# One of the four weight sums of each group made by an adding transfer that GpSimd begins

## The chip, the cores and the metric

The kernel runs on one core of one Trainium2 chip. The core has five engines that this text speaks of by these names: TensorE (PE in the profile; its weight loads are PEld), VectorE (DVE), ScalarE (ACT), GpSimd (POOL) and SyncE (SP), which here only begins transfers. Sixteen DMA engines move the data. Each engine works through its own list of instructions in order; semaphores make one wait for another.

The metric is the device time of one execution in microseconds. Three runs of the kernel before took 2479.81, 2481.71 and 2482.42 us; their median is 2481.71 us.

## The reference

Two blocks of a transformer are computed on 512 tokens of width 1024, in float32. Of the first block only the two SwiGLU layers matter here (the first layer of the block and the third):

```python
def swiglu(y, w_gate, w_up, w_down):
    return (jax.nn.silu(y @ w_gate) * (y @ w_up)) @ w_down
```

`w_gate` and `w_up` are 1024 x 2816, `w_down` is 2816 x 1024. Between the two SwiGLU layers stands a token mixer with two recurrences (mLSTM and HGRN2). The second block has a neighbourhood attention, a differential attention, two convolutional feed-forward layers and two small gated layers.

## The kernel before, in words

**Every float32 product is three fast products.** A weight tile is rounded to a fast format (`wh`, by ScalarE) and the rest is kept beside it (`wl`, by VectorE); activations are split the same way into `yh` and `yl`. TensorE then adds up wh·yh, wh·yl and wl·yh.

**The gate and up products of the SwiGLU layers** save a multiplication of blocks: `seven` forms a block of 256 output rows by seven products of half blocks instead of eight (Strassen's scheme). For that the weights must be summed beforehand. `sums_w` does this for one group, that is 256 columns of one matrix. The four quarters of the group are a, b, c and d (each 128 x 512 in SBUF), and the sums are s1 = c + d, s2 = s1 - a, s3 = a - c and s4 = b - s2. A group takes three tiles of the pool `wraw` (tag `wr`, four buffers): x[0] holds a and s1, x[1] holds s2 and b, x[2] holds d and c; s3 takes c's place and s4 takes a's. Three transfers on SP's queue bring c and d (one of 512 KB), a and b (256 KB each). VectorE makes the four sums. Then the halves of (a, s1), (s2, b), (d, s3) and (s4) are written into the pool `wts` (tags `wh` and `wl`, six buffers each): that is what TensorE reads.

A group is 7 x 4 x 3 = 84 multiplications of 256 columns. In each of the two SwiGLU layers there are 19 such groups (one block of `w_gate` is done in the ordinary way), so 38 in all. After every second block pair (four groups), `partial` multiplies by a part of `w_down`: four ordinary weight tiles with 24 multiplications of 512 columns each. Those tiles pass through the same `wr` and `wts` buffers.

**What sets the order.** All operations are first recorded with tiles as dependencies. `deadlines` works backwards from an estimated time for each TensorE operation and gives every other operation a latest start; a transfer's is moved forward by 40 us more (`DMA_AHEAD`). It also orders the tiles of the first-come pools (`wr`, `wh`, `wl`, `ps`) by when they are first due. `schedule` then runs a list scheduler with fixed prices, picks on each engine the operation that is due first and whose buffers are free, and `emit` writes the instructions out in that order. Every engine's list is therefore fixed at build time: an instruction that waits on the chip holds back all that stand behind it on its engine. All instructions written by `emit` carry one line (L514 before, L515 after).

`SLOTS` fixes how many buffers each pool has; the pool `acts` holds activations of 128 x 516 floats and has 56.

Of the kernel before, what the change touches and what calls it, by code (L numbers as in the profile page):

```python
# [13 lines left out]
ALU = mybir.AluOpType  # L14
# [25 lines left out]
class Tile_:  # L40


    def __init__(self, rec, pool, tag, shape, dt, name):
        self.rec, self.pool, self.tag, self.shape, self.dt, self.name = rec, pool, tag, list(shape), dt, name
        self.real = None
        self.uses = 0
        self.acc = []
        n = int(np.prod(shape[1:]))
        self.np = np.lib.stride_tricks.as_strided(rec.dummy, (shape[0], n), (rec.width, 1)).reshape(shape) if len(shape) == 2 else None
        self.made = False  # L50
        self.turn = None
        self.n = None
        self.last = None


class View:
# [116 lines left out]
DMA_AHEAD = 40000.0  # L173
# [13 lines left out]
class Recorder:  # L187
# [59 lines left out]
    def add(self, eng, fn, args, kw):  # L247
        o = Op()
        o.i, o.eng, o.fn, o.args, o.kw = len(self.ops), eng, fn, args, kw
        views = [a for a in list(args) + list(kw.values()) if isinstance(a, View)]  # L250
        out = kw.get("out", args[0] if args else None)
        outs = [v for v in (out, kw.get("accum_out")) if isinstance(v, View)]
        ins = [v for v in views if not any(v is w for w in outs)]
        if fn in ("copy_predicated",) or (fn == "matmul" and not kw.get("start")):
            ins = ins + [outs[0]]
        o.cost = self.price(eng, fn, outs[0] if outs else None, args, kw, ins)
        o.lat = 0.0
# [4 lines left out]
        if fn == "dma_start":  # L262
            v = outs[0] if outs else ins[0]
# [8 lines left out]
        if eng == "tensor":  # L272
            t = outs[0].t
# [29 lines left out]
    def deadlines(self, slots, when):  # L303

        ops = self.ops
        late = {}
        tiles = {}
        for o in ops:
            for t in o.tiles:
                if t.pool in self.psum:  # L310
                    q = tiles.setdefault(t.tag, [])
                    if t.n is None:
                        t.n = len(q)
                        q.append(o)
                    t.end = o
        need = {}
        for o in ops:
            for t in o.tiles:
                if t.pool in self.psum and t.end is o:
                    q = tiles[t.tag]  # L320
                    j = t.n + slots[t.pool, t.tag]
                    if j < len(q):
                        need[o.i] = min(need.get(o.i, 1e18), when[q[j].i] - 230)
        for o in reversed(ops):
            end = min([late[u.i] - WAIT[o.eng][u.eng] - (SLACK.get(o.outn.split("_")[0], SLACK[""]) if o.eng != u.eng else 0.0) for u in o.users] + [need.get(o.i, 1e18)], default=1e18)
            if o.fn == "dma_start":
                end -= 2100 + DMA_AHEAD
            s = end - o.cost
            if o.eng == "tensor":
                s = min(s, when[o.i])  # L330
            elif s > 1e17:
                s = when[o.i] + 20000.0
            if o.fn == "dma_start":
                s = o.pr if not o.users or o.kept else min(s, o.pr)
            late[o.i] = o.pr = s
        first = {}
        for o in reversed(ops):
            for x in o.tiles:
                first[id(x)] = late[o.i]
        for q in self.fifo.values():  # L340
            for i, x in enumerate(sorted(q, key=lambda x: first[id(x)])):
                x.turn = i

    def schedule(self, slots, reserve):
# [11 lines left out]
        tfree = dict.fromkeys(engs, 0.0)  # L356
# [12 lines left out]
        now = 0.0  # L369
        done = 0  # L370
        n = len(ops)
# [20 lines left out]
        while done < n:  # L392
# [4 lines left out]
            for e in engs:  # L397
# [3 lines left out]
                while w and w[0][0] <= now:  # L401
                    _, i, o = heapq.heappop(w)
# [4 lines left out]
                while r:  # L407
                    x = heapq.heappop(r)
                    o = x[2]
# [29 lines left out]
                o = pick  # L439
# [10 lines left out]
                c = o.cost  # L450
# [9 lines left out]
                if o.fn == "dma_start":  # L460
                    s = max(now + 500, dma_free)
                    dma_free = s + c
                    o.end = dma_free + 1600
                    tfree[e] = now + 450
                else:
                    o.end = now + c
                    tfree[e] = o.end
# [29 lines left out]
            now = min(nxt)  # L497
# [17 lines left out]


SLOTS = {
    ("acts", "a"): 56, ("wraw", "wr"): 4, ("pads", "pad"): 3, ("wts", "wh"): 6, ("wts", "wl"): 6,
    ("pmm", "mm"): 4, ("pat", "at"): 2, ("paux", "aux"): 2,
}  # L520
RESERVE = {("acts", "a"): 12}
# [29 lines left out]
class Builder:  # L551
# [169 lines left out]
    def sums_w(self, key, g):  # L721

        nc = self.nc
        W = self.I["s_" + key[0]][g]
        n = 4 * P
        nc.offset = -LOOK_DMA
        x = [nc.tile("wraw", "wr", [P, WP], F32, self.nm("wr"), True) for _ in range(3)]
        h = slice(0, n), slice(n, 2 * n)
        a, s1, s2, b, d, c = [t[:, i] for t in x for i in h]
        nc.sync.dma_start(out=x[2][:, 0:2 * n], in_=W[:, 2 * n:4 * n])  # L730
        nc.sync.dma_start(out=a, in_=W[:, 0:n])
        nc.sync.dma_start(out=b, in_=W[:, n:2 * n])
        nc.offset = -LOOK_PREP
        forms = {}

        def halves(t, names):
            hi = nc.tile("wts", "wh", [P, WP], F32R, self.nm("wh"), True)
# [4 lines left out]
                nc.scalar.copy(out=hi[:, i], in_=t[:, i])  # L742
                nc.vector.tensor_tensor(out=lo[:, i], in0=t[:, i], in1=hi[:, i].bitcast(F32), op=ALU.subtract)

        nc.vector.tensor_tensor(out=s1, in0=c, in1=d, op=ALU.add)
        nc.vector.tensor_tensor(out=s2, in0=s1, in1=a, op=ALU.subtract)
        nc.vector.tensor_tensor(out=c, in0=a, in1=c, op=ALU.subtract)
        halves(x[0], ("a", "s1"))
# [1144 lines left out]
```

## Time and profile before

| what | value |
|---|---|
| median of three runs | 2481.71 us |
| the profiled execution | 2484.38 us |
| its span | 2482.6 us |
| granted TensorE clock, mean share | 0.991 |
| PE busy | 2403.4 us (97%) |
| DVE busy | 1838.7 us (74%) |
| ACT busy | 1159.6 us (47%) |
| POOL busy | 459.3 us (18%) |
| moved by DMA | 270.37 MB, 109 GB/s |

The span is the time from the first to the last instruction of the program; 1.8 us of the profiled execution lie around it. A busy share is an average over stages with different limits. In rows of the trace, "ps", "wh", "wr" and so on are tiles without their buffer numbers; "idle before" is how long an engine stood still just before an instruction, with the instruction or transfer that ended the wait.

### The profile page before, as it was taken

The page shows a single profiled execution, that of the slowest core. Times are in us where ns is not written, and L with a number is a line of the kernel's source. Part 1 is how long each engine was busy: PE and PEld are TensorE (multiplying, and loading weights), DVE is VectorE, ACT ScalarE, POOL GpSimd, SP SyncE. Part 2 cuts the span into 40 slices and gives each one's busy share as a digit, 9 for nine tenths or more (in the row PEclk, how much of TensorE's full clock was granted, in tenths as well). Part 3 has the DMA queues.
Part 4 walks back from the last instruction along what each step waited for, and adds up shares of the span by engine and source line. Part 5 has one row for each costly group of instructions (what it writes and reads, how often), then busy time and mean ns, then how long its engine had stood idle before and what let it go on. Part 6 is the DMA issues. An engine that isn't in the chain of part 4 may idle for free.

```text
span 2482.6 us, 37567 instructions
## 1 busy us (share of the span) xinstructions
PE 2403.4 (97%) x14452; PEld 2107.3 (85%) x14452; DVE 1838.7 (74%) x3100; ACT 1159.6 (47%) x2084; POOL 459.3 (18%) x549
## 2 busy tenths in 40 slices
PE   9999999998999999989999999999999999999999
PEld 6899999987789999987779888789877788888788
DVE  8988878873768877787887872667888879744567
ACT  5544444142535444546665442334565565433343
POOL 1000003000130000055543210113223223100122
PEclk9999999999999999999999999999999999999999
DMA  9644444574225433422322323233312223333322
GB/s 332 210 154 151 132 124 84 114 157 99 94 58 172 137 103 102 153 65 64 93 62 78 111 94 94 93 95 109 99 49 84 67 77 102 94 94 97 93 93 75
DMA packets 227925, 270.37 MB, mean 109 GB/s; under 512 B 10769, under 2 KB 191249, under 8 KB 227746
## 3 DMA queue, kind: packets, MB, share of 16 engines
q1 hardware_dynamic: 227746, 267.98, 35.9%
q8 instruction: 113, 1.85, 0.3%
q14 instruction: 66, 0.54, 0.1%
HBM read 261.62 MB, written 10.51 MB: 110 GB/s over the span
## 4 chain that ended last, share of the span: by engine, by line
PE 40%; DVE 7%; issue 2%; ACT 1%; POOL 1%; POOLq 0%; DVEq 0%; ACTq 0%
PE ps L514 36%; DVE wl L514 1%; DVE P L514 1%; PE sc L514 1%; PE po L514 1%; DVE z L514 1%; DVE h L514 1%; DVE ul L514 1%; DVE Kl L514 1%; PE pt L514 1%; ACT P L514 0%; POOL P L514 0%; PE ss L514 0%; POOL rsq L514 0%; DVE yl L514 0%
## 5 line engine op out<-in xcount | busy, mean ns | idle before, releaser
L514 PE MATMUL ps<-yl,wh 128*128 128x256 f32 (+1 forms) x2528 | 793.1, 321 | 6.3 <-DVE yl L514 6.2
L514 PE MATMUL ps<-yh,wh 128*128 128x256 f32 (+1 forms) x2528 | 784.5, 321 | 13.7 <-ACT yh L514 8.0
L514 PE MATMUL ps<-yh,wl 128*128 128x256 f32 (+1 forms) x2528 | 787.7, 320 | 0.0
L514 DVE TENSOR_TENSOR wl<-wr,wh 128x1024 fp32r<-128x1024 f32 x466 | 562.2, 1210 | 231.0 <-ACT wh L514 228.9
L514 ACT CAST wh<-wr 128x1024 fp32r<-128x1024 f32 x466 | 468.5, 1012 | 534.6 <-PE ps L514 387.9
L514 PEld LDWEIGHTS ps<-yh,wh 128*128 128x128 f32 x2528 | 472.1, 190 | 54.2 <-ACT yh L514 11.7
L514 PEld LDWEIGHTS ps<-yl,wh 128*128 128x128 f32 x2528 | 474.1, 190 | 47.1 <-DVE yl L514 12.1
L514 PEld LDWEIGHTS ps<-yh,wl 128*128 128x128 f32 x2528 | 474.2, 190 | 34.4
L514 PE MATMUL ps<-uh,wh 128*128 128x512 f32 (+1 forms) x1336 | 481.8, 367 | 9.8 <-DVE z L514 7.4
L514 PE MATMUL ps<-ul,wh 128*128 128x512 f32 (+1 forms) x1336 | 484.1, 366 | 3.8 <-DVE ul L514 3.8
L514 PE MATMUL ps<-uh,wl 128*128 128x512 f32 (+1 forms) x1336 | 483.4, 366 | 0.0
L514 POOL TENSOR_TENSOR sq<-sq,sq 128x256 f32<-128x256 f32 (+1 forms) x150 | 137.1, 917 | 841.6 <-ACT sq L514 838.8
L514 PEld LDWEIGHTS ps<-uh,wh 128*128 128x128 f32 x1336 | 250.2, 189 | 50.1 <-issue 3.0
L514 PEld LDWEIGHTS ps<-ul,wh 128*128 128x128 f32 x1336 | 252.1, 189 | 42.6 <-DVE ul L514 4.3
L514 PEld LDWEIGHTS ps<-uh,wl 128*128 128x128 f32 x1336 | 251.7, 189 | 38.4
L514 POOL TENSOR_TENSOR cx<-cx,cv 128x512 f32<-128x512 f32 x44 | 76.5, 1758 | 558.7 <-DVE cv L514 535.6
L514 DVE TENSOR_TENSOR z<-z,ps 128x256 f32<-128x256 f32 (+1 forms) x176 | 88.8, 513 | 103.3 <-PE ps L514 102.6
L514 DVE SCALAR_TENSOR_TENSOR ada<-ada,scb 128x1024 f32<-128x1024 f32 x72 | 88.5, 1234 | 24.7 <-DMA ada<-in_adaT_dram 24.6
L514 POOL TENSOR_SCALAR P<-P,sm 128x256 f32<-128x256 f32 (+2 forms) x96 | 72.9, 777 | 140.2 <-DVE sm L514 115.0
L514 ACT ACTIVATE P<-P,mx 128x512 f32<-128x512 f32 (+2 forms) x128 | 81.1, 635 | 31.9 <-DVE mx L514 25.7
L514 ACT ACTIVATE sq<-z 128x256 f32<-128x256 f32 x112 | 45.6, 416 | 96.5 <-DVE z L514 95.9
L514 DVE TENSOR_TENSOR wr<-wr 128x512 f32<-128x512 f32 x114 | 78.3, 687 | 6.3 <-DMA wr<-in_s_ffn_w_up_dram 4.3
(238 smaller groups left out, 3163.3 us busy)
## 6 DMA issues: line engine op xcount, KB each, us to landing
wr<-in_ffn_w_in_dram SPq DMA_DIRECT2D x88, 512.0 KB, 3.6
ada<-in_adaT_dram SPq DMA_DIRECT2D x72, 512.0 KB, 6.4
wr<-in_ffn_w_down_dram SPq DMA_DIRECT2D x44, 512.0 KB, 4.3
wr<-in_ffn_w_out_dram SPq DMA_DIRECT2D x44, 512.0 KB, 3.4
wr<-in_w_in_dram SPq DMA_DIRECT2D x32, 512.0 KB, 9.1
wr<-in_na_w_qkv_dram SPq DMA_DIRECT2D x24, 512.0 KB, 3.9
wr<-in_da_w_qkv_dram SPq DMA_DIRECT2D x24, 512.0 KB, 3.8
wr<-in_s_ffn_w_up_dram SPq DMA_DIRECT2D x20, 512.0 KB, 4.2
```

Source lines behind the costliest of these rows:

```text
L514: getattr(getattr(nc, o.eng), o.fn)(*[real(a) for a in o.args], **{k: real(v) for k, v in o.kw.items()})
```

## The change

In `sums_w` the sum s1 = c + d is no longer made by VectorE. SP loads d a second time, into the place of s1, and then GpSimd begins a transfer that reads c from memory a second time and adds it to what lies there (`accum_op=ALU.add`). That transfer reads and writes s1, so it is ordered behind the load of d into s1. Each group now reads 512 KB more.

Three things go with it. The three tiles of a group are made "mates": in the order of the `wr` pool they stand together, in the place of the one that is due first, so x[0], x[1], x[2] now follow one another, where x[2] came first. A transfer begun by GpSimd gets its own price and latest start. And the memory set aside for the lists of transfers that GpSimd writes grows from 1024 to 4096 (`dynamic_dma_scratch_size`), while the pool `acts` shrinks from 56 to 54 buffers.

```diff
@@ class Tile_
         self.last = None
+        self.mates = [self]
@@ Recorder.add
-        if fn in ("copy_predicated",) or (fn == "matmul" and not kw.get("start")):
+        if fn in ("copy_predicated",) or (fn == "matmul" and not kw.get("start")) or "accum_op" in kw:
             ins = ins + [outs[0]]
@@ Recorder.deadlines
             if o.fn == "dma_start":
-                end -= 2100 + DMA_AHEAD
+                end -= 2100 + (DMA_AHEAD if o.eng == "sync" else 1000)
...
-            if o.fn == "dma_start":
+            if o.fn == "dma_start" and o.eng == "sync":
                 s = o.pr if not o.users or o.kept else min(s, o.pr)
...
-            for i, x in enumerate(sorted(q, key=lambda x: first[id(x)])):
+            for i, x in enumerate(sorted(q, key=lambda x: min(first[id(y)] for y in x.mates))):
@@ Recorder.schedule
-                    tfree[e] = now + 450
+                    tfree[e] = now + (450 if e == "sync" else 1000)
@@ SLOTS
-    ("acts", "a"): 56, ("wraw", "wr"): 4, ("pads", "pad"): 3, ("wts", "wh"): 6, ("wts", "wl"): 6,
+    ("acts", "a"): 54, ("wraw", "wr"): 4, ("pads", "pad"): 3, ("wts", "wh"): 6, ("wts", "wl"): 6,
@@ Builder.sums_w
         x = [nc.tile("wraw", "wr", [P, WP], F32, self.nm("wr"), True) for _ in range(3)]
+        for t in x:
+            t.t.mates = [v.t for v in x]
...
         nc.sync.dma_start(out=x[2][:, 0:2 * n], in_=W[:, 2 * n:4 * n])
+        nc.sync.dma_start(out=s1, in_=W[:, 2 * n:3 * n])
         nc.sync.dma_start(out=a, in_=W[:, 0:n])
         nc.sync.dma_start(out=b, in_=W[:, n:2 * n])
         nc.offset = -LOOK_PREP
         forms = {}
+        nc.gpsimd.dma_start(out=s1, in_=W[:, 3 * n:4 * n], accum_op=ALU.add)
...
-        nc.vector.tensor_tensor(out=s1, in0=c, in1=d, op=ALU.add)
         nc.vector.tensor_tensor(out=s2, in0=s1, in1=a, op=ALU.subtract)
@@ kernel
-    nc = bacc.Bacc("TRN2", target_bir_lowering=False, num_devices=1, dynamic_dma_scratch_size=1024)
+    nc = bacc.Bacc("TRN2", target_bir_lowering=False, num_devices=1, dynamic_dma_scratch_size=4096)
```

The first place is VectorE's list in the middle of the first SwiGLU layer, where one group (x[0] to x[2] are wr_1573, wr_1597, wr_1540) ends and the next (wr_1713, wr_1722, wr_1632) begins. Before:

```order
L514 TENSOR_TENSOR wr_1540<-wr_1573,wr_1540 128x512
L514 TENSOR_TENSOR z_999<-z_999,ps_1637 128x512
L514 TENSOR_TENSOR z_1004<-z_1004,ps_1661 128x512
L514 TENSOR_TENSOR wr_1573<-wr_1597 128x512
L514 TENSOR_TENSOR wl_1711<-wr_1540,wh_1697 128x1024
L514 TENSOR_TENSOR wr_1713<-wr_1632 128x512
L514 TENSOR_TENSOR wr_1722<-wr_1713 128x512
L514 TENSOR_TENSOR z_1038<-z_1038,ps_1699 128x512
L514 TENSOR_TENSOR z_1043<-z_1043,ps_1704 128x512
L514 TENSOR_TENSOR wl_1754<-wr_1573,wh_1741 128x512
L514 TENSOR_TENSOR wr_1632<-wr_1713,wr_1632 128x512
```

VectorE's list at the same place, with the groups (wr_1563, wr_1580, wr_1606) and (wr_1638, wr_1722, wr_1730), now:

```order
L515 TENSOR_TENSOR wr_1606<-wr_1563,wr_1606 128x512
L515 TENSOR_TENSOR z_1006<-z_1006,ps_1642 128x512
L515 TENSOR_TENSOR z_1012<-z_1012,ps_1668 128x512
L515 TENSOR_TENSOR wr_1563<-wr_1580 128x512
L515 TENSOR_TENSOR wl_1719<-wr_1606,wh_1705 128x1024
L515 TENSOR_TENSOR wr_1722<-wr_1638 128x512
L515 TENSOR_TENSOR z_1035<-z_1035,ps_1707 128x512
L515 TENSOR_TENSOR z_1046<-z_1046,ps_1712 128x512
L515 TENSOR_TENSOR wl_1758<-wr_1563,wh_1749 128x512
L515 TENSOR_TENSOR wr_1730<-wr_1638,wr_1730 128x512
```

The sum s1 (wr_1713<-wr_1632 before) is gone; s2 (wr_1722<-wr_1638) and s3 (wr_1730<-wr_1638,wr_1730) keep their places.

SP's list for the same groups, with two tiles of `w_down` ahead, before:

```order
L514 DMA wr_1506<-in_ffn_w_down_dram 128x4x256
L514 DMA wr_1540<-in_s_ffn_w_gate_dram 128x1024
L514 DMA wr_1573<-in_s_ffn_w_gate_dram 128x512
L514 DMA wr_1597<-in_s_ffn_w_gate_dram 128x512
L514 DMA wr_1632<-in_s_ffn_w_up_dram 128x1024
L514 DMA wr_1713<-in_s_ffn_w_up_dram 128x512
L514 DMA wr_1722<-in_s_ffn_w_up_dram 128x512
```

SP's list at the same place, now ("x2" is the load of d into s1 and the load of a):

```order
L515 DMA wr_1499<-in_ffn_w_down_dram 128x4x256
L515 DMA wr_1563<-in_s_ffn_w_gate_dram 128x512 x2
L515 DMA wr_1580<-in_s_ffn_w_gate_dram 128x512
L515 DMA wr_1606<-in_s_ffn_w_gate_dram 128x1024
L515 DMA wr_1638<-in_s_ffn_w_up_dram 128x512 x2
L515 DMA wr_1722<-in_s_ffn_w_up_dram 128x512
L515 DMA wr_1730<-in_s_ffn_w_up_dram 128x1024
```

x[0] now takes the first buffer that comes free and x[2], with c and d, the last.

GpSimd's list around the start of the second SwiGLU layer, now: before, the first DMA row and the eighteen that follow the last `rsq` here were not there.

```order
L515 TENSOR_TENSOR sq_7410<-sq_7410,sq_7530 128x256
L515 DMA wr_7491<-in_s_ffn_w_up_dram 128x512
L515 TENSOR_TENSOR rsq_7628<-ms_7620,mhalf 128x2
L515 TENSOR_TENSOR sq_7663<-sq_7663,sq_7669 128x256
L515 TENSOR_TENSOR sq_7663<-sq_7663,sq_7686 128x256
L515 TENSOR_TENSOR sq_7663<-sq_7663,sq_7692 128x256
L515 TENSOR_TENSOR sq_7663<-sq_7663,sq_7709 128x256
L515 TENSOR_TENSOR sq_7663<-sq_7663,sq_7715 128x256
L515 TENSOR_TENSOR rsq_7767<-ms_7761,mhalf 128x2
L515 DMA wr_8233<-in_s_ffn_w_gate_dram 128x512
```

One adding transfer stands ahead of a reciprocal root (`rsq`); in the first layer all 19 stand in one piece with no other work of GpSimd among them. Outside the SwiGLU layers the lists are the same but for two stretches, one in each attention of the second block, where PE, ACT and DVE have some of their rows in another order.

## Rows read from the trace of the kernel before

**Rows 1.** The page's busy line: us, share of the span, instructions.
```profile
PE 2403.4 (97%) x14452; PEld 2107.3 (85%) x14452; DVE 1838.7 (74%) x3100; ACT 1159.6 (47%) x2084; POOL 459.3 (18%) x549
```

**Rows 2.** Stretches: busy us of PE, PEld, DVE, ACT, POOL; PEclk, DMA share, GB/s.
```profile
0.00:73.00 73.00, 65.06 (x255) 47.92 (x256) 61.55 (x118) 39.50 (x59) 10.09 (x10) 1.00 0.95 332
...
100.00:300.00 200.00, 200.00 (x1379) 185.52 (x1378) 173.54 (x265) 89.05 (x137) 0.00 (x0) 1.00 0.47 155
...
690.00:780.00 90.00, 84.42 (x652) 80.59 (x650) 73.81 (x149) 45.17 (x85) 21.41 (x24) 0.96 0.41 119
780.00:1040.00 260.00, 259.67 (x1834) 242.67 (x1835) 208.25 (x301) 126.32 (x195) 0.00 (x0) 1.00 0.37 118
1160.00:1260.00 100.00, 96.60 (x500) 78.22 (x501) 80.48 (x170) 64.13 (x149) 55.62 (x65) 1.00 0.25 76
1850.00:1950.00 100.00, 97.33 (x527) 80.33 (x526) 85.56 (x182) 60.87 (x121) 28.28 (x22) 1.00 0.26 82
```

**Rows 3.** Timeline of PE in a group: start, duration; first and 27th row.
```profile
199.81 0.29 PE L514 MATMUL ps<-yl,wh 128*128 128x256 f32 x1
...
202.88 0.28 PE L514 MATMUL ps<-yh,wh 128*128 128x256 f32 x1
```

**Rows 4.** Timeline of PE in a tile of w_down, four starts apart.
```profile
149.01 0.39 PE L514 MATMUL ps<-yh,wh 128*128 128x512 f32 x1
...
149.94 0.40 PE L514 MATMUL ps<-yl,wh 128*128 128x512 f32 x1
```

**Rows 5.** Waits, 100 to 300 us: total us, times, longest.
```profile
ACT wh L514 <- PE ps L514: 70.3, 35, 5.0
...
DVE wr L514 <- DMA wr<-in_s_ffn_w_up_dram: 4.3, 3, 1.4
```

**Rows 6.** Tile wr, 100 to 300 us: durations min/median/max in ns.
```profile
L514 ACT CAST wh<-wr x64: 619/1049/1059, 99.4 to 297.8; 128x1024 fp32r<-128x1024 f32 x51, 128x512 fp32r<-128x512 f32 x13
...
DMA to landing us min/median/max: 2.8/3.7/8.5
```

**Rows 7.** Timeline of DVE around both rsq: idle by the first, busy by the second.
```profile
705.68 0.48 DVE L514 SCALAR_TENSOR_TENSOR z<-z,G,R 128x256 f32<-128x256 f32 x1 [1.47 <-PE R L514]
...
728.22 1.22 DVE L514 TENSOR_TENSOR wl<-wr,wh 128x1024 fp32r<-128x1024 f32 x1
```

**Rows 8.** The page's groups: sums in SBUF on DVE.
```profile
L514 DVE TENSOR_TENSOR wr<-wr 128x512 f32<-128x512 f32 x114 | 78.3, 687 | 6.3 <-DMA wr<-in_s_ffn_w_up_dram 4.3
```

**Rows 9.** Waits of PE, 15 to 100 us; then 690 to 780 us.
```profile
PE ps L514 <- ACT yh L514: 3.9, 3, 2.7
...
PE ps L514 <- ACT yh L514: 3.3, 2, 3.0
PE R L514 <- POOL rsq L514: 1.6, 3, 0.8
```

**Rows 10.** DMA issues: KB each, median us from issue to landing.
```profile
wr<-in_s_ffn_w_up_dram SPq DMA_DIRECT2D x20, 512.0 KB, 4.2
wr<-in_s_ffn_w_up_dram SPq DMA_DIRECT2D x40, 256.0 KB, 3.0
...
t5rep<-t5vec SPq DMA_DIRECT2D x8, 511.5 KB, 10.9
```

**Rows 11.** Timeline of DVE from one group's last split to the next's.
```profile
197.27 0.68 DVE L514 TENSOR_TENSOR wl<-wr,wh 128x512 fp32r<-128x512 f32 x1
...
220.57 0.69 DVE L514 TENSOR_TENSOR wr<-wr 128x512 f32<-128x512 f32 x1 [1.43 <-DMA wr<-in_s_ffn_w_up_dram]
...
222.37 0.68 DVE L514 TENSOR_TENSOR wl<-wr,wh 128x512 fp32r<-128x512 f32 x1
```

**Rows 12.** Timeline of POOL, 702 to 745 us: two of its rows.
```profile
704.29 0.71 POOL L514 TENSOR_TENSOR rsq<-ms,mhalf 128x2 f32<-128x2 f32 x1 [3.15 <-DVE ms L514]
...
727.99 2.01 POOL L514 TENSOR_TENSOR rsq<-ms,mhalf 128x2 f32<-128x2 f32 x1 [4.24 <-DVE ms L514]
```

**Rows 13.** Timeline of SP: the second layer's first group load.
```profile
720.04 0.34 SPq L514 DMA_DIRECT2D wr<-in_s_ffn_w_up_dram  x1
```

## The prediction

> **What bounds the kernel now.** I read the busy line first, then the busy time by stretch for the places that the change touches, and only then single rows. TensorE is busy 97% of the span and VectorE 74% [rows 1], but these are averages over stages, so the question is who ends last in the two SwiGLU layers. By stretch, PE is busy 200.00 of 200 us in the first layer's middle and 259.67 of 260 in the second's, while VectorE is busy 173.54 (87%) and 208.25 (80%) [rows 2]. A busy PE need not be at its peak, so the reader should look at starts: from the first to the 27th row of a group 3.07 us pass, 26 steps of 118 ns for 256 columns [rows 3]; in a tile of w_down four steps take 0.93 us, 232 ns for 512 columns [rows 4]. Both come to 0.46 ns a column, at a granted clock of 1.00 [rows 2], so it is one steady pace, without holes. Nothing that makes VectorE lighter can make this stretch shorter.
>
> The rows that say who waits agree. In 200 us ScalarE's casts into wh stood still 70.3 us, at 35 of 64 casts, until PE had freed a buffer [rows 5, 6]: the weights are made as far ahead as the six buffers allow. VectorE's sums waited 4.3 us in all for a transfer [rows 5], and a PE that is busy 200.00 of 200 us waits for nothing. So the stage has spare time on VectorE already, and a cover between it and PE. A tile of wts feeds 24 multiplications or 24 x 0.118 = 2.8 us of PE; with five tiles ready ahead that is 14.2 us, less a cast of 1.05 [rows 6] and a split of 1.22 [rows 7], some 11.9 us.
>
> **The change part by part.**
>
> *Removed:* 38 of the 114 rows wr<-wr, at 687 ns each [rows 8]: 26.1 us of VectorE. Of these, 34 lie where PE is full, and are worth nothing there. Four lie at the starts of the two layers, two groups each, where PE does wait: 65.06 us busy of 73 at the first, 84.42 of 90 at the second [rows 2], for yh above all (3.9 and 3.3 us [rows 9]), which hangs on VectorE's work. Only the sum of the first group stands ahead of such a wait; I count one sum at each start, 2 x 0.69 = 1.4 us gained. If the waits for yh all went with it, 7.2 us would be the other end; if VectorE's list is otherwise no better, 0.
>
> *Added, the second load of d:* 38 on SP's queue. A load of 256 KB lands 3.0 us after its issue [rows 10]. It is issued with a and goes into x[0], which now takes the first buffer that comes free. By the rule of the list that is the buffer of x[0] of the group before last (three tiles a group, four buffers), so a whole group's preparation lies between this load and the first cast that needs s1. PE needs 84 x 0.118 = 9.9 us for a group, and with the four tiles of w_down (24 x 0.232 = 5.6 us each) it takes 62.0 us for four groups, 15.5 on average. VectorE's rows show the long case: 25.1 us between the last split of one group and that of the next [rows 11].
>
> *Added, the adding transfer:* 38 on GpSimd's queue. No row of before shows such a transfer, nor any that GpSimd begins. From below: a plain 256 KB load lands in 3.0 us [rows 10]. From above: the slowest large transfer lands in 10.9 us [rows 10]; that one is memory to memory in a crowded queue, and with 2.0 us for GpSimd's part [rows 12] it is 12.9. It has two inputs and one output, so I go by the row of 512 KB, 4.2 us, and add 0.7 for GpSimd's own start, as long as a small operation of it takes [rows 12]: 4.9 us, say 5. Load and addition then take 3.0 + 5 = 8.0 us, under the 9.9 us of the tightest case, and hidden. The Trainium skill's page "DMA: Bandwidth & Descriptors", section "Anatomy of one DMA — SWDGE (gpsimd) path", gives such transfers some 2.0 us and the bytes at 436 GB/s, so as an estimate from that page 2.6 us for 256 KB; by it the chain would be shorter still and the sum the same. No run here shows it yet.
>
> *What waits behind it.* On GpSimd's list the 19 transfers of the first layer stand alone, and nothing is behind them until the layer's end. At the start of the second layer one stands between an sq and an rsq on which TensorE waits (R after rsq: 1.6 us [rows 9]). SP issues that group's first load at 720.04 us [rows 13] and the rsq begins at 727.99 [rows 12], so 3.0 us to land and a GpSimd start of 0.7 to 2.0 still leave it clear; I cost it at nothing, and at 2.0 us if not. On VectorE's list s2 and s3 wait for transfers: s3 now needs x[2], whose 512 KB (4.2 us [rows 10]) can be fetched only when the previous x[2] has been split. Four instructions of about 0.69 us stand between, so VectorE will stand still 4.2 - 2.8 = 1.4 us there, about as long as it now does for a (1.43 us [rows 11]). One small wait takes the place of another, under the same cover.
>
> *Added bytes:* 38 x 512 KB = 19.9 MB in some 550 us, 36 GB/s. The DMA engines are busy 0.47 at 155 GB/s [rows 2]; in proportion that becomes 0.58. Free, except in the first 73 us at 0.95 and 332 GB/s, where 0.5 MB of the first group cost up to 1.6 us of transfer time; VectorE, not the transfers, is full in that part, so I take 0 and keep 1.6 as an end.
>
> *Moved:* two stretches in the attentions, because two acts buffers are gone. PE is idle 3.4 us in the one and 2.7 us in the other [rows 2]. No direction follows from the list: 0, with ends of -3 (half of that idle gone) and +6 (it doubles).
>
> The sum is -1.4 us against the profiled execution's 2484.38: 2483.0. That execution is 2.67 us above the median 2481.71, so for a median I forecast **2480.3 us**, in effect no change. About 0.2% (5 us) is what a measurement of this kernel can tell from none.
>
> **The rivals.**
>
> *The addition comes late (slower).* Place: the first cast of each group, which needs a and s1. It decides from the point where load and addition exceed 9.9 us by more than the cover spreads over four groups: 9.9 + 11.9 / 4 = 12.9 us, an addition of 9.9 us. At 10.5 us (13.5 in all) four groups lose 4 x 3.6 - 11.9 = 2.5 us, and with 38 / 4 = 9.5 such rounds 24 us: 2506. At the upper end of 12.9 (15.9 in all) it is 12.1 x 9.5 = 115 us: 2597. For it speaks that GpSimd is disturbed by VectorE: the same rsq takes 0.71 us while VectorE stands still and 2.01 beside a split [rows 7, 12], and VectorE is 87% busy in this stage. Against it: tripling GpSimd's 0.7 gives 9.4 us in all, still under 9.9. The Trainium skill ("SBUF — State Buffer", section "Who interferes with whom") says that a two-input VectorE operation holds off only GpSimd instructions that read SBUF, and infers that writing transfer lists needs the write side alone. By that rule GpSimd's part would stay near 0.7 us; the trace agrees with the first half of it (rsq reads SBUF), and no row shows the second.
>
> *The order got worse (slower).* Fewer acts buffers, the moved stretches, the rsq behind a transfer and the crowded start: 6 us at most from the attentions, 2.0 and 1.6 from the others. Some two thirds of that is 6 us: 2488.
>
> *VectorE's time counts at the edges (faster).* Both waits for yh shrink by half, 3.6 us, and the attentions gain 3: 2475. For it: VectorE is busy 61.55 of the first 73 us [rows 2] and stands on the way to yh. Against it: only one sum is ahead of each wait.
>
> *VectorE bounds the layers after all (faster).* Then all 26.1 us come back: 2456. Against it stands the pace of 118 ns without a hole.
>
> **How the numbers follow.** The forecast's case 0.55 (2476 to 2485), late addition 0.12, worse order 0.15, edges 0.15, VectorE-bound 0.03. A range of 2473 to 2500 leaves out the last, the far part of the late addition (0.09) and a few of the edges: 0.17. Faster by over 0.2% (under 2476.7): 0.05 of the forecast's case, 0.13 of the edges, 0.03: 0.21. Slower (over 2486.7): 0.04 of the forecast's, 0.12 late, 0.11 of the order: 0.27. The rest, 0.52, is no change.
>
> **What the profile after should show.** 76 rows wr<-wr instead of 114, VectorE about 26 us less busy and PE as long busy as before; 100 to 300 us still full at 118 ns a start; SP issuing 38 more loads; the adding transfers landing about 5 us after GpSimd issues them; casts still waiting for PE at about half of their number. Wrong would be: PE waiting on a cast wh at the head of groups (late addition), VectorE's s2 waiting long for a GpSimd transfer, or more idle PE time in the two attention stretches than 3.4 and 2.7 us.

## The result, and the profile after

The change makes the kernel slower. Four runs of the kernel after took 2497.53 to 2501.14 us, median **2499.7 us**; four runs of the kernel before beside them took 2479.81 to 2482.59, median 2482.07. The ratio is **1.0072**, with a 95% interval of 1.0055 to 1.009. The forecast was 2480.3, no change; 2499.7 lies just inside its range of 2473 to 2500, but far from its likeliest case. The profiled execution has a span of 2498.3 us, against 2482.6 before.

The page's busy line and the sums on VectorE, now (for rows 1 and 8):

```profile
PE 2409.7 (96%) x14452; PEld 2110.4 (84%) x14452; DVE 1816.5 (73%) x3062; ACT 1159.3 (46%) x2084; POOL 494.3 (20%) x587
```
```profile
L515 DVE TENSOR_TENSOR wr<-wr x76: 679/686/694, 63.1 to 1045.1; 128x512 f32<-128x512 f32 x76
```

The 38 sums are gone from VectorE, which is 22.2 us less busy (1838.7 before; the sums' own rows make 26.1, other rows took somewhat longer), and GpSimd is 35.0 us busier with 38 more rows. Where the time went shows in the stretches. The columns are those of [rows 2]:

```profile
100.00:300.00 200.00, 192.95 (x1308) 177.05 (x1307) 158.02 (x239) 86.70 (x133) 10.33 (x12) 0.98 0.62 187
690.00:780.00 90.00, 83.57 (x641) 80.78 (x641) 67.97 (x139) 40.18 (x78) 23.70 (x25) 0.94 0.39 113
780.00:1040.00 260.00, 255.22 (x1770) 235.25 (x1769) 190.90 (x280) 122.52 (x187) 15.57 (x18) 1.00 0.52 150
1160.00:1260.00 100.00, 96.66 (x501) 78.24 (x500) 81.37 (x169) 65.47 (x149) 53.28 (x62) 1.00 0.26 80
1850.00:1950.00 100.00, 95.66 (x550) 80.49 (x549) 84.43 (x163) 55.44 (x112) 30.72 (x25) 1.00 0.20 62
```

PE was busy 200.00 of 200 us in the first SwiGLU layer and is now idle 7.05 us there, with 1308 multiplications begun instead of 1379. In the second layer it is idle 4.78 instead of 0.33. The stretch between them (690 to 780 us) and the two in the attentions lie within 1.7 us of before. A steadier measure than busy time is the delay of the same work: both traces hold 14,452 multiplications, so the k-th of the one can be set against the k-th of the other. At these starts in the trace before, the same multiplication after the change is later by (us):

```
start before     15    73   100   125   160   200   225   300   500   600   780   800   860   920   980  1040  2470
later after    -0.4   1.4   0.0   4.4   6.2   6.1  10.0  11.4  11.8   8.7   9.0   9.4  11.4  13.2  15.3  15.3  15.9
```

So 11.4 us are lost between 100 and 300 us and 6.3 between 780 and 1040, in steps: one of 4.4 us near 117 us, and then one of 1.4 to 4 us in each round of four groups and a part of `w_down`, some 64 us apart (near 155, 219 and 285 us, and near 852, 916 and 980). (The 3 us won back between 500 and 600 are won as well in the traces of three kernels below that are no faster than before, 2.7 to 4.1 us in experiments 1, 3 and 4; nothing is built on them.)

**What happens in one such step.** Waits from 100 to 300 us, now (for rows 5: total us, times, longest):

```profile
ACT wh L515 <- PE ps L515: 59.4, 30, 4.9
ACT wh L515 <- DMA wr<-in_s_ffn_w_gate_dram: 12.5, 3, 4.7
...
DVE wr L515 <- issue: 7.5, 3, 3.1
...
PE ps L515 <- DVE o L515: 2.6, 1, 2.6
PE ps L515 <- ACT yh L515: 2.4, 3, 1.3
PE ps L515 <- DVE yl L515: 2.1, 3, 0.7
```

No line has PE waiting for a cast or a split of weights (wh, wl), and ScalarE's casts still wait 59.4 us for PE: the cover of weights holds. PE waits for o, yh and yl, the *activations*. The reason is in the timeline of the first round's end (start, duration, engine; the idle time before a row in brackets):

```profile
144.32 4.01 SPq L515 DMA_DIRECT2D wr<-in_s_ffn_w_gate_dram  x4
...
148.05 0.86 POOL L515 DMA_DIRECT2D wr<-in_s_ffn_w_gate_dram  x1 [20.26 <-DVE wl L515]
...
148.50 1.05 ACT L515 CAST wh<-wr 128x1024 fp32r<-128x1024 f32 x1 [0.97 <-PE p L515]
...
150.72 0.41 DVE L515 TENSOR_TENSOR o<-o,ps 128x256 f32<-128x256 f32 x1
...
153.53 0.69 DVE L515 TENSOR_TENSOR wr<-wr 128x512 f32<-128x512 f32 x1 [2.40 <-issue]
153.61 2.00 ACT L515 CAST wh<-wr 128x1024 fp32r<-128x1024 f32 x2 [4.06 <-DMA wr<-in_s_ffn_w_gate_dram]
...
154.14 0.42 DVE L515 TENSOR_TENSOR o<-o,ps 128x256 f32<-128x256 f32 x1
154.47 1.02 DVE L515 TENSOR_TENSOR o<-o,o 128x256 f32<-128x256 f32 x2
...
155.53 1.14 ACT L515 CAST yh<-o 128x512 fp32r<-128x512 f32 x2
...
156.20 0.73 PE L515 MATMUL ps<-yh,wh 128*128 128x512 f32 x2 [0.63 <-ACT yh L515]
156.88 1.29 DVE L515 TENSOR_TENSOR yl<-o,yh 128x512 fp32r<-128x512 f32 x2
157.62 0.50 PE L515 MATMUL ps<-yl,wh 128*128 128x512 f32 x1 [0.69 <-DVE yl L515]
```

Read it from the top. SP begins the load of d into s1 at 144.32; GpSimd begins the adding transfer at 148.05, 3.7 us later; it lands at 153.46, another 5.4 us later, and s1 is whole. (The row puts the end of GpSimd's wait down to a split by VectorE that had just ended. In the 26 of the 38 groups whose load of d has a landing in the trace, GpSimd begins 0.56 us after it as a median, so the load is the likelier end here too.) At that moment two engines go on at once: VectorE with s2 = s1 - a, after 2.40 us of nothing, and ScalarE with the cast of (a, s1), after 4.06. "Issue" means that the profile shows no releaser; that it is the addition, the first experiment below shows. Behind s2 in VectorE's list stand the evacuations o, and behind these on ScalarE yh, on VectorE yl. They need nothing of the new weights. PE needs them for the next multiplications of `w_down`, and stops twice, for 1.0 and 1.1 us less the normal 0.23 us of a step.

The transfers (KB each, median us from the start of the issue to landing; for rows 10; at the six heads of rounds, from 148 to 973 us, the additions took 5.3 to 6.3 us):

```profile
wr<-in_s_ffn_w_up_dram SPq DMA_DIRECT2D x60, 256.0 KB, 3.7
...
wr<-in_s_ffn_w_up_dram POOLq DMA_DIRECT2D x20, 256.0 KB, 4.2
wr<-in_s_ffn_w_gate_dram POOLq DMA_DIRECT2D x18, 256.0 KB, 4.7
```

**The price of a stop beyond itself.** At 117 us the longest stop of the two layers comes in a group's own multiplications: from 116.94 to 119.85 PE starts nothing and waits for o. The stretches around it, and last the one with the two stops of 1 us seen above:

```profile
100.00:116.90 16.90, 16.90 (x109) 15.28 (x108) 14.69 (x25) 8.70 (x14) 0.86 (x1) 1.00 0.77 217
116.90:120.00 3.10, 0.47 (x4) 0.26 (x3) 3.10 (x9) 0.17 (x1) 0.00 (x0) 1.00 0.36 58
120.00:124.00 4.00, 4.00 (x22) 4.00 (x23) 2.67 (x4) 3.04 (x5) 0.00 (x0) 0.57 0.93 339
124.00:128.00 4.00, 4.00 (x36) 4.00 (x36) 3.31 (x5) 2.06 (x4) 0.86 (x1) 1.00 0.90 338
155.00:165.00 10.00, 8.68 (x37) 6.41 (x36) 8.44 (x12) 2.72 (x4) 0.57 (x1) 1.00 0.30 70
```

After the stop the granted clock falls to 0.57 on average from 120 to 124 us: 16 steps there take 213 ns instead of 118, which is TensorE's lower level of 1.2 GHz instead of 2.4, and then the pace is back. The stop (2.9 us less one step) costs another 16 x 0.095 = 1.5 us. After the two short stops the clock stays at 1.00.

This stop too goes back for the most part to an addition, by a longer way. The one begun at 89.63 lands at 95.26; ScalarE's cast waits for it, VectorE's next split waits for that cast, and VectorE, busy 14.69 of the 16.9 us in the first row above, does not make this good:

```profile
95.42 1.05 ACT L515 CAST wh<-wr 128x1024 fp32r<-128x1024 f32 x1 [5.75 <-DMA wr<-in_s_ffn_w_gate_dram]
...
96.50 1.23 DVE L515 TENSOR_TENSOR wl<-wr,wh 128x1024 fp32r<-128x1024 f32 x1 [3.31 <-ACT wh L515]
```

Set against the same rows of the first experiment below, which has no additions, VectorE is 1.1 us later just ahead of this split, 4.5 from it on, and 5.0 at the evacuation at 119.38, for which PE waits. Of what lies between, 1.51 us is a wait for another load (ada, 0.68 there) and 0.35 us s2's own wait. In the first layer the seven stops of over 0.3 us make 8.2 us, and this 1.5; the other 1.7 of the 11.4 lie in smaller steps that I did not sort.

### The profile page after: what moved, and what is told of

It is laid out like the page before. It is cut to its first block, busy times and chain, and to the rows that moved or that the text cites. A ratio compares the mean times of both kernels' runs of the same rounds, so it can differ in the third digit from the quotient of the medians.

```text
span 2498.3 us, 37689 instructions
## 1 busy us (share of the span) xinstructions
PE 2409.7 (96%) x14452; PEld 2110.4 (84%) x14452; DVE 1816.5 (73%) x3062; ACT 1159.3 (46%) x2084; POOL 494.3 (20%) x587
## 3 DMA queue, kind: packets, MB, share of 16 engines
q0 software_dynamic: 5472, 9.96, 2.4%
## 4 chain that ended last, share of the span: by engine, by line
PE 71%; DVE 16%; DMA 5%; issue 4%; ACT 3%; POOL 1%; SPq 0%; POOLq 0%; ACTq 0%; DVEq 0%
PE ps L515 62%; DVE wl L515 3%; DMA wr<-in_s_ffn_w_gate_dram 2%; DVE h L515 2%; DVE z L515 2%; DVE P L515 2%; PE p L515 2%; PE sc L515 2%; PE po L515 1%; DMA ada<-in_adaT_dram 1%; DVE ada L515 1%; PE pt L515 1%; DVE Kl L515 1%; PE hl L515 1%; DVE ul L515 1%
## 5 line engine op out<-in xcount | busy, mean ns | idle before, releaser
L515 DVE SCALAR_TENSOR_TENSOR ada<-ada,scb 128x1024 f32<-128x1024 f32 x72 | 88.5, 1236 | 22.2 <-DMA ada<-in_adaT_dram 22.1
L515 POOL DMA_DIRECT2D wr<-in_s_ffn_w_gate_dram x18 | 15.6, 866 | 351.6 <-DMA wr<-in_s_ffn_w_gate_dram 179.0
```

Source lines behind the costliest of these rows:

```text
L515: getattr(getattr(nc, o.eng), o.fn)(*[real(a) for a in o.args], **{k: real(v) for k, v in o.kw.items()})
```

## The experiments

**My theory (T)**, after the two traces: the lists are fixed at build time, and the scheduler believed that the addition ends 2.9 us after its issue (0.5 + 0.8 + 1.6 in its model). It takes 4.2 to 4.7 as a median and up to 7.8. So s2 and the cast stand too early in two lists, wait there, and hold back the activations. Rivals: the second load of d crowds SP's transfers (R1); the order and the smaller acts pool (R2); the adding in the transfer itself (R3); a small price at every addition rather than at the round's heads (R4).

**1. The additions left out, the order kept.**

```diff
 for o in self.order:
+    if "accum_op" in o.kw:
+        continue
```

> The changed kernel with the 38 adding transfers left out when the instructions are written; every list keeps the order of the changed kernel otherwise (s1 holds d alone, so the s1 and s2 products are left without c). Theory (T): VectorE's s2 and ScalarE's cast of (a, s1) stand in the list where the scheduler thinks the addition is done, wait for it at the head of each round of four groups, and hold back o, yh and yl behind them, for which PE waits. Then without the addition some 18 us come back in the two SwiGLU layers: 2478 to 2484, the waits of PE for yh, yl and o at the heads gone. Rival (R1), the second load of d: 10 MB more on SP's queue slow its loads; that load is still there, so 2494 or more. Rival (R2), order: 54 acts buffers and the moved lists cost it; 2495 to 2500.

Measured: 2481.84 us, ratio to before 0.9996 (0.9987 to 1.0005). All of the loss is gone; the second load, the 54 acts buffers and the new lists cost nothing that can be measured by themselves, which leaves R1 and R2 next to nothing. (The second load still counts as the first part of the chain that ends with the addition; no run has the addition without it.) The waits of 12.5 us (ScalarE's casts for a transfer of w_gate) and of 7.5 us (VectorE's sums, "issue") are gone, so both were waits for the addition. Its stretches of the two layers, with PE full again:

```profile
100.00:300.00 200.00, 200.00 (x1391) 185.97 (x1390) 166.17 (x253) 89.78 (x137) 0.00 (x0) 1.00 0.51 171
780.00:1040.00 260.00, 260.00 (x1854) 243.94 (x1853) 196.59 (x283) 127.20 (x195) 0.00 (x0) 1.00 0.42 138
```

It also gives the ceiling of the idea. Here VectorE has lost its 38 sums and nobody waits for anything instead, and the kernel is no faster than before: the 26 us of VectorE were worth nothing that can be measured against it.

**2. A plain transfer instead of an adding one.**

```diff
 for o in self.order:
+    o.kw.pop("accum_op", None)
```

> The changed kernel with the GpSimd transfers as plain ones: the same 256 KB of c are written over d in s1, nothing is added (s1 is c, not c + d). Same order, same dependences. T: it is the latency of a transfer begun by GpSimd behind a first load that counts; if the adding makes little of it, a plain one lands in 3.5 to 4 us after GpSimd's 0.9 us instead of 4.2 to 4.7, and each of the heads waits 0.5 us less: 2494 to 2499. Rival (R3), the adding itself (read and write of SBUF in the transfer): then the plain transfer lands in 2.5 to 3 us and most comes back: 2483 to 2490. R1 and R2: no change, 2499.

Measured: 2491.24 us, ratio 1.0031 (1.0021 to 1.0042): between what T and R3 expected. The adding costs more than I had thought, and a plain transfer begun by GpSimd is still too late. Its issues land in 3.3 and 3.4 us, 0.9 and 1.3 us sooner, and GpSimd itself is done sooner (busy us, mean ns of one in the page's groups, here and then in the kernel after):

```profile
wr<-in_s_ffn_w_up_dram POOLq DMA_DIRECT2D x20, 256.0 KB, 3.3
wr<-in_s_ffn_w_gate_dram POOLq DMA_DIRECT2D x18, 256.0 KB, 3.4
...
L516 POOL DMA_DIRECT2D wr<-in_s_ffn_w_gate_dram x18 | 9.7, 540 | 347.7 <-DMA wr<-in_s_ffn_w_gate_dram 152.1
```
```profile
L515 POOL DMA_DIRECT2D wr<-in_s_ffn_w_gate_dram x18 | 15.6, 866 | 351.6 <-DMA wr<-in_s_ffn_w_gate_dram 179.0
```

About 1.1 us less in each of 38 / 4 = 9.5 rounds would be 10 us; 2499.7 - 2491.2 = 8.5 came back. The trace does not show it so evenly: the stops of over 0.3 us in the two layers come to 6.3 us, against 14.2 in the kernel after; the one at 117 us, 4.3 us with its slow steps, is gone, those at the heads are shorter, and two of 1.2 and 0.9 us at 131 and 138 us are new. The 38 x 256 KB of GpSimd's queue are moved in both, so the bytes are not it.

**3. Only what goes along with the change.**

```diff
-            for i, x in enumerate(sorted(q, key=lambda x: first[id(x)])):
+            for i, x in enumerate(sorted(q, key=lambda x: min(first[id(y)] for y in x.mates))):
...
-    ("acts", "a"): 56, ("wraw", "wr"): 4, ...
+    ("acts", "a"): 54, ("wraw", "wr"): 4, ...
...
+        for t in x:
+            t.t.mates = [v.t for v in x]
...
-    ... dynamic_dma_scratch_size=1024)
+    ... dynamic_dma_scratch_size=4096)
```

> The kernel before with only what goes along with the change: the three tiles of a group as mates, 54 acts buffers, 4096 instead of 1024 for the transfer lists; VectorE makes s1 as before, no second load. T: 2479 to 2486, within 0.2% of before. R2 (order and buffers): 2492 to 2500.

Measured: 2485.09 us, ratio 1.0009 (1.0001 to 1.0018). At most a small part (up to some 4 us) of the 17.6 us; PE is full in both layers (200.00 of 200 and 260.00 of 260 us). Whether this 0.09% is real against the 0.9996 of the first experiment, which holds the same side edits, is not settled: the intervals overlap. The medians of the two kernels lie 3.3 us apart: so much at most would the sums be worth under these side edits, and part of it can be the order of the lists, which differs.

**4. The scheduler told what an addition takes.**

```diff
-                    o.end = dma_free + 1600
+                    o.end = dma_free + (1600 if e == "sync" else 5600)
...
-                end -= 2100 + (DMA_AHEAD if o.eng == "sync" else 1000)
+                end -= 2100 + (DMA_AHEAD if o.eng == "sync" else 5000)
```

> The changed kernel whose scheduler is told what the addition takes: in its model the transfer ends 4 us later (6.9 instead of 2.9 us after its issue), and its latest start lies 4 us earlier. Same work, other lists: s2 and the cast of (a, s1) stand behind the evacuations and splits that are due meanwhile. T: the waits in front of o, yh and yl go, 2480 to 2488, and PE's gaps at the heads vanish. R1 and R3 (the transfers themselves are too slow for the buffers): 2495 or more, with PE then waiting for wh.

Measured: 2483.71 us, ratio 1.0009 (1.0 to 1.0018), as T expected. The transfers, their number and the buffers are those of the kernel after; only the latest start of the additions, the place of s2, the casts and what hangs on them in the lists is another, and 16 of the 17.6 us are back. The additions come no sooner: from the start of the load of d to the landing of the addition the 38 groups take 9.5 us as a median, against 9.1 in the kernel after. The stops at the heads are gone; five others of 0.6 to 2.0 us stand elsewhere in the two layers (near 203, 213, 276, 781 and 964 us):

```profile
100.00:300.00 200.00, 196.95 (x1350) 181.47 (x1349) 162.35 (x244) 88.37 (x136) 12.06 (x14) 1.00 0.62 187
780.00:1040.00 260.00, 258.38 (x1819) 240.95 (x1818) 197.46 (x286) 126.19 (x194) 14.68 (x17) 1.00 0.52 153
```

**5 and 6. Which additions?** The sum given back to VectorE in every second group of `w_gate` (10 of 38, among them the heads of the rounds), and the reverse.

```diff
+        add = not ("gate" in key[0] and g % 2 == 0)   # the reverse: without "not"
+        if add:
+            nc.sync.dma_start(out=s1, in_=W[:, 2 * n:3 * n])
...
+        if add:
+            nc.gpsimd.dma_start(out=s1, in_=W[:, 3 * n:4 * n], accum_op=ALU.add)
...
+        if not add:
+            nc.vector.tensor_tensor(out=s1, in0=c, in1=d, op=ALU.add)
```

> The changed kernel, with the sum s1 given back to VectorE (and no second load) in 10 of the 38 groups: every second group of w_gate, among them each one that follows the four tiles of w_down; 28 adding transfers stay. T: only the heads of rounds meet a late addition, since only there are the buffers of the last three tiles held by w_down until shortly before; the stops of PE at 155, 219, 285, 790, 852, 916 and 980 us go, the one at 117 us (2.8 us and 1.6 us of half clock) stays or moves: 2483 to 2488. Rival (R4): every addition costs a little (38 alike); then 28 of 38 of the 18 us stay: 2495.

> The reverse: adding transfers only in those 10 groups, the other 28 sums by VectorE without a second load. T: the stops at the heads stay, 1.5 to 2.5 us each at seven or eight places: 2493 to 2498. R4: 10 of 38 of the 18 us, 2486 to 2487.

Measured: heads by VectorE 2488.46 us (just above T's 2488), ratio 1.0023 (1.0013 to 1.0033); heads alone by additions 2495.77 us, ratio 1.0051 (1.0038 to 1.0063). By the ratios the ten additions alone cost some 70% of the loss, the other 28 alone some 30% (each kernel has lists of its own): R4 falls, which had 1.005 and 1.002 for them, the other way round. But "only the heads" is too narrow as well. In the first layer the 28 cost almost nothing; in the second they stop PE at 822 us for 2.7 us, in the middle of a round:

```profile
100.00:300.00 200.00, 199.09 (x1375) 184.58 (x1374) 167.84 (x252) 90.70 (x139) 8.60 (x10) 1.00 0.58 181
780.00:1040.00 260.00, 256.11 (x1788) 237.87 (x1788) 197.46 (x288) 123.64 (x189) 11.26 (x13) 1.00 0.47 140
```

**7 and 8. A fifth raw weight buffer**, for the kernel after and, as its control, for the kernel before.

```diff
-    ("acts", "a"): 54, ("wraw", "wr"): 4, ...     # before: 56 and 4
+    ("acts", "a"): 52, ("wraw", "wr"): 5, ...
```

> The changed kernel with five raw weight buffers instead of four and 52 acts buffers instead of 54. T: at the head of a round x[0] gets its buffer one w_down tile (24 x 232 ns = 5.6 us) earlier, more than the addition is late, so the stops in the SwiGLU layers go: 2479 to 2487 if two acts buffers more cost little elsewhere. Rival (R5), the place in the list alone counts and not the buffer (the scheduler moves s2 and the cast forward with the buffer): 2494 or more, with the stops where they were.

> Control of the last: the kernel before with five raw weight buffers and 52 acts buffers. T: PE was already full in both SwiGLU layers, so nothing is gained there: 2479 to 2487, the difference from the last one showing what the addition still costs with five buffers. Rival: earlier loads help the first 73 us or the waits for yh at 690 to 780 us: 2470 to 2476.

Measured: with the additions 2494.94 us, ratio 1.005 (1.0038 to 1.0063); the control 2478.82, ratio 0.9987 (0.9979 to 0.9996). My expectation for the first missed, and its rival R5 came out in time, though the stops lie elsewhere (the longest, of 2.0 to 2.8 us, near 149, 843 and 909 us). Beside its control it loses 0.63%, nearly as much as the kernel after with four buffers. The buffer did come earlier: SP begins the load of d at 138.03 instead of 144.32. But the scheduler moved s2 forward with it, and VectorE now stands still for more than twice as long (2.40 us in the kernel after):

```profile
138.03 5.50 SPq L515 DMA_DIRECT2D wr<-in_s_ffn_w_gate_dram  x4
...
142.14 0.86 POOL L515 DMA_DIRECT2D wr<-in_s_ffn_w_gate_dram  x1 [21.21 <-DVE wl L515]
...
148.59 0.69 DVE L515 TENSOR_TENSOR wr<-wr 128x512 f32<-128x512 f32 x1 [5.34 <-issue]
```

This addition lands at 148.51, 5 us sooner than in the kernel after, but s2 begins to wait 7.9 us sooner (143.25 instead of 151.13). So an earlier buffer alone does not remove the loss; what counts is the reader's place in the list against the landing. The control is the only kernel here that is faster than before, by 0.13%, and it has nothing of the change.

**9 to 11. Both together, and the dose the other way.** Five buffers with 4 us more in the model, and with 7 more; and the kernel after with 1.5 us *less* in the model:

```diff
-                    o.end = dma_free + 1600
+                    o.end = dma_free + (1600 if e == "sync" else 5600)   # with 5 buffers; and 8600; alone: 100
...
-                end -= 2100 + (DMA_AHEAD if o.eng == "sync" else 1000)
+                end -= 2100 + (DMA_AHEAD if o.eng == "sync" else 5000)   # with 5 buffers; and 8000; alone: as it was
```

> Five raw weight buffers, 52 acts buffers, and the scheduler told that the addition ends 4 us later. The earlier runs showed that either way alone leaves something: with five buffers the scheduler moved s2 forward by as much as the buffer came earlier, and VectorE waited 5.34 us. T (what counts is the place in the list against the landing): both together leave no late addition, 2477 to 2483, as the kernel before with five buffers (2478.8). Rival (R6), five buffers crowd the transfers by themselves: then 2488 or more, with long landings of SP's loads at the stops.

> As the first of these three, with 7 us more in the scheduler's model instead of 4. T: no wait for an addition is left, so nothing more is gained, 2477 to 2483; if at 4 us more some additions are still late, this one is 2 to 6 us faster than that. If the model now puts s2 so late that the casts come late, PE waits for wh: 2486 or more.

> The dose the other way: the changed kernel, its scheduler told that the addition ends 1.5 us earlier (1.4 instead of 2.9 us after its issue). Same work, same buffers, same transfers. T: s2 and the cast of (a, s1) stand up to 1.5 us earlier in the lists and wait that much longer, at some eight to ten places: 2503 to 2514. If the number in the scheduler's model is not the cause but the transfers are, 2497 to 2502.

Measured: 2483.31 us, ratio 1.0004 (0.9996 to 1.0013); with 7 us more 2483.28, ratio 1.0005 (0.9996 to 1.0014); with 1.5 less **2528.95**, ratio 1.0188 (1.0174 to 1.0202). The first two differ from the kernel before by nothing that can be measured (their own expectation, 2477 to 2483, just missed); beside the control with five buffers they are, by the ratios, 4 us slower. What these 4 us are is open. The traces show how many of VectorE's sums begin right after the landing of an addition for which VectorE stood still (within 0.25 us of it), and how long it stood in all: 16 and 28.1 us in the kernel after, 17 and 53.6 us with 1.5 us less in the model, 3 and 2.8 us with 4 us more (experiment 4), none in either of these two with five buffers (ScalarE's casts still stand so three times, 2.4 us each, with 4 us more, and never with 7). The dose went the expected way and far beyond the size that I gave it: 29 us more than the kernel after, not 3 to 14. By the delay of the same work the two layers lose 49 us here against 17.7; the stops of over 0.3 us make 33.7 of it, against 14.2, and 86 steps of 256 columns that take about 213 ns add some 8. The chains are as long as in the kernel after (9.1 us as a median in both). The earlier place also makes additions late that were in time before. One of them, at 128 us (the timeline of all engines; PE starts nothing from 128.13 to 134.00):

```profile
125.31 0.86 POOL L515 DMA_DIRECT2D wr<-in_s_ffn_w_up_dram  x1 [15.62 <-DMA wr<-in_s_ffn_w_up_dram]
...
128.13 0.28 PE L515 MATMUL ps<-yh,wl 128*128 128x256 f32 x1
132.93 0.69 DVE L515 TENSOR_TENSOR wr<-wr 128x512 f32<-128x512 f32 x1 [6.04 <-DMA wr<-in_s_ffn_w_up_dram]
133.06 1.05 ACT L515 CAST wh<-wr 128x1024 fp32r<-128x1024 f32 x1 [6.90 <-DMA wr<-in_s_ffn_w_up_dram]
133.54 0.41 DVE L515 TENSOR_TENSOR o<-o,ps 128x256 f32<-128x256 f32 x1
...
134.00 0.58 PE L515 MATMUL ps<-yh,wh 128*128 128x256 f32 x1 [5.59 <-DVE o L515]
```

Here the profile names the releaser: both engines wait for the transfer into s1, which lands at 132.90, 7.6 us from its issue; the next row of VectorE is the evacuation o, and PE waits for that. After this stop steps of 256 columns take 213 ns again. Its two layers, with a granted clock of 0.94 and 0.98:

```profile
100.00:300.00 200.00, 180.61 (x1229) 167.92 (x1228) 145.43 (x221) 82.80 (x128) 9.49 (x11) 0.94 0.56 171
780.00:1040.00 260.00, 247.62 (x1676) 228.49 (x1676) 186.44 (x279) 116.50 (x176) 13.03 (x15) 0.98 0.50 145
```

## Why the prediction was wrong

**Right: what bounds the kernel, and what VectorE's sums are worth.** PE's steady pace in the two layers said that a lighter VectorE buys nothing; the first experiment, 26 us of sums gone and no time won, agrees with it. The 1.4 us gained at the starts can't be seen: the same multiplication at 73 us starts 1.4 us later, and at 100 us at the same time.

**The sum 3.0 + 5 = 8.0: right for most additions, too small for the chain.** I said 5 us for the addition from 4.2 and 0.7; its median is 4.2 to 4.7, with 0.87 of it on GpSimd. The plain load was 3.0 in my sum; the medians are 3.5 and 3.7 now, with 38 more loads and the additions beside it. But between the landing of that load and the start of GpSimd's transfer lie another 0.56 us (median of the 26 groups that show it), for which my sum had nothing, and at the six heads the additions took 5.3 to 6.3 us. From the start of the load of d to the landing of the addition the 38 groups took 7.8 to 12.9 us, 9.1 as a median; nine took longer than my 9.9, all of them elsewhere, and the six heads 9.1 to 9.9. The Trainium skill's "DMA: Bandwidth & Descriptors" (section "Anatomy of one DMA — SWDGE (gpsimd) path"), from which I had the estimate of 2.6 us, does not agree: even a plain one took 3.3.

GpSimd's part of a transfer did not grow beside VectorE: 857 to 865 ns in all twelve transfers from 100 to 300 us, beside a VectorE busy 79% of the time, and in the second experiment 536 to 547 ns in 35 of 38, one of them (903.79 us, 545 ns) with VectorE standing still; the other three took 581, 626 and 764 ns, which I did not explain. The Trainium skill's "SBUF — State Buffer" (section "Who interferes with whom") infers that the writing of transfer lists is not held off by two-input operations of VectorE; the traces agree.

**Wrong, step 1: the time that the chain has.** "A whole group's preparation lies between this load and the first cast that needs s1", 9.9 us in the tightest case. I took the tightest case from PE's shortest group. But x[0] takes the first buffer that comes free, and at a round's head the buffers before it belong to the four tiles of `w_down`; the load goes out at 144.32. The cast of (a, s1) stands right behind the cast that ends at 149.55. That is 5.2 us, not 9.9, for a chain of 9.1 us; the difference of 3.9 us, and 0.15 until the cast begins, is the 4.06 that ScalarE waited.

**Wrong, step 2, and this one decided: what stands behind the wait.** For the late case I had given the price as PE lacking weights, after a cover of 11.9 us. The cover held, as forecast; PE never waited for a wh. I had asked what is queued behind the new transfer on GpSimd's list, and for VectorE's new wait I reasoned that it lies "under the same cover". But VectorE's and ScalarE's lists carry the evacuations and the splits of activations as well, and these have almost no cover. In the kernel before, at the same multiplications:

```profile
149.58 1.14 ACT L514 CAST yh<-o 128x512 fp32r<-128x512 f32 x2
...
150.23 1.29 DVE L514 TENSOR_TENSOR yl<-o,yh 128x512 fp32r<-128x512 f32 x2
...
151.10 0.62 PE L514 MATMUL ps<-yh,wh 128*128 128x512 f32 x2
...
151.57 0.40 PE L514 MATMUL ps<-yl,wh 128*128 128x512 f32 x1
```

The second of the two yl ends at 151.52 and PE goes on with yl at 151.57; the casts into yh end at 150.20 and 150.72 and PE takes the first at 151.10. So a wait of 2.4 us on VectorE and 4.06 on ScalarE reached PE as two stops, together 1.6 us more than two normal steps, at a chain of 9.1 us, far below the 12.9 us from which I had let lateness count. Experiments 1, 4 and 10 show this step: the addition away, the same addition with its readers later, and with its readers earlier, give 2481.8, 2483.7 and 2529.0 us. It is not the wait of s2 as such: at 321.46, 889.19, 953.22 and 1016.97 us s2 waits 2.2 to 2.5 us as well, while ScalarE loses at most 1.0 us there, and PE stops at most 0.3 us longer than a step. Whether it is VectorE's wait or ScalarE's that PE feels at the heads, no run separates.

**The rivals.** "The addition comes late" had the right cause, with its place nearly right (the heads of rounds, rather than of each group), and the wrong victim and price; its own point of decision would have excluded it at the 9.1 us measured (37 of the 38 chains lie below its 12.9, one at 12.92). "The order got worse" is not it: 1.0009 at most, and the two attentions neither gained nor lost (15.6 us behind at 1160, 15.3 at 1260; 14.8 at 1850 and at 1950). What I named as a sign against myself, s2 waiting long for a GpSimd transfer, is what the trace shows; PE waiting on a cast, the other sign, is not. That 2499.7 still lies inside the range is luck: the range was drawn for a worse order of the lists and for additions later than these.

**The rsq behind a transfer** cost nothing, as forecast: GpSimd's one such transfer begins at 733.64 and its next rsq, at 737.84, waits for ms. PE does wait 2.2 us for an rsq in that stretch, but as long in the first experiment, where no transfer is left.

## What to carry to other kernels

A cover is a property of one consumer, not of an engine: before an instruction is given a new wait, list what stands behind it in its engine's list, and take the *smallest* cover among those, not that of the data that the instruction itself makes. Where a scheduler writes the order, its price for a new kind of operation is part of the change; 1.5 us too little in the model cost here 29 us, and 4 us more gave back nearly all, while an earlier buffer alone gave back some 5 of 17.6. And work taken off an engine that is not the bound was worth nothing here that could be measured against the kernel before, so any price for it was a loss.

## What was not expected of the hardware

- A 256 KB transfer begun by GpSimd takes 3.3 to 3.4 us plain and 4.2 to 4.7 us adding (medians), and GpSimd spends 540 ns on the one and 866 on the other (means). The adding ones take 5.3 to 6.3 us at the six heads of rounds, where SP begins the 512 KB load of the same group within 0.5 us of them; whether that is why, no run shows. GpSimd begins 0.56 us after the landing that it waits for (median of 26). The queue's packets go from 3040 to 5472 for the same 9.96 MB.
- After 2.9 us without a start PE ran 16 steps at 213 instead of 118 ns, half its clock. After the stops of about 1 us at 155 and 157 us the granted clock stayed at 1.00, and in the fifth experiment it stayed there after one of 2.8 us (821.93 to 824.76) as well: stops of nearly the same length need not cost the same.
